# First tile after three norms from unsplit float32 products of x (1 + scale) and shift

## The chip, the cores and the metric

The kernel runs on one core of a Trainium2 chip. The metric is the time of one execution on the device in microseconds (us); a verdict compares repeated executions of the two kernels on the same chip. The core's engines work side by side and meet through semaphores: PE (matrix products, with its weight loads shown as PEld), DVE (elementwise work), ACT (elementwise work with functions), POOL, and SP, whose queue issues nearly all transfers. Each engine takes its instructions in the order of its own program. Products are summed in PSUM, eight banks of 512 float32 columns.

## The reference

A two-layer decoder trunk on 256 tokens of width 1024. Each layer has a token mixer (layer 0 a mixture of three attentions, layer 1 a gated linear attention, GLA) and a gated feed-forward part. Before each of the four sub-layers stands a norm with a shift and scale from a conditioning vector:

```python
sh1, sc1, g1, sh2, sc2, g2 = split(silu(c) @ w_ada[i] + b_ada[i])
h = rmsnorm(x, norm_mix[i]) * (1.0 + sc1) + sh1
...
x = x + g1 * y
h = rmsnorm(x, norm_ffn[i]) * (1.0 + sc2) + sh2
x = x + g2 * conv_ffn(h, w_up[i], conv_w[i], conv_b[i], w_down[i])
```

`rmsnorm(x, g)` is `x * rsqrt(mean(x * x) + eps) * g`. The mean is taken over the 1024 channels of a token, so its factor (called r below, `rstd` in the code) is one number per token. Hence, for a weight matrix W, `h @ W = r * ((x * g * (1 + sc)) @ W) + sh @ W`: the factor r can be applied before or after the product.

## The kernel before

**Layout.** Everything is channel-major: x is held as eight tiles x[kt] of 128 channels by 256 tokens, and an activation stands in the same form. A weight tile of 128x2048 (1 MB) is loaded by SP's queue into one of four buffers `raw`.

**Products in three parts.** The engine's faster float32 format (fp32r) keeps fewer bits, so each float32 operand is split in two: `split` (line 154) casts a weight tile on ACT to `whi` (two instructions of 1024 columns) and puts the rest on DVE into `wlo` (two more). There are three buffers for `whi` and three for `wlo`. `mm3` (line 171) then makes three fp32r matmuls, hi*hi, hi*lo and lo*hi, which appear in the profile as lines 174, 175 and 176. A tile of `w_up`, `w_qk_b` or `w_r_b` takes 48 matmuls of 256 columns.

**A norm.** While the last projection of a sub-layer runs, `residual` (line 271) updates x[kt] on DVE, and `add_square` (line 194) squares it on ACT and adds the squares up in three partial sums. `all_normed` (line 265) calls `rstd_of` (line 182): three matmuls with a matrix of 1/1024 sum the partial sums over the channels (`ms`), and ACT makes ln and then exp of it (`ln`, `rstd`). Behind them six matmuls of nothing (`warm`) run. `normed` (line 245) makes for each of the eight kt `xr = x * scale * r` on DVE (line 250), `hhi = xr + shift` on ACT (line 252) and `hlo`, the rest, on DVE (line 253). Then the products of the next sub-layer may start with h[0].

**Three of the norms.** Norm A stands between the output projection of the attention (`project`, line 515, tiles `py`) and the feed-forward part of layer 0; norm B between the down projection of layer 0 (tiles `pd`) and the GLA; norm C between `project` of the GLA and the feed-forward part of layer 1. The norm at the very start is another piece of code.

**Feed-forward part.** `ffn` (line 538) first makes 22 tiles of `w_up` (i = 0 to 21): 48 matmuls into one bank `pab`, then on ACT and DVE a convolution over three tokens (`r`), silu, a product and its split into `ghi` and `glo`. Every third (layer 0) or fifth (layer 1) tile brings a piece of the conditioning (`next_ada`), a 1 MB load and two long DVE reductions (`ada_raw`, line 138). Then 32 half tiles of `w_down` follow (`pd`).

**GLA.** After norm B come the values (`pv`, 96 matmuls of 512 columns over four tiles of `w_v_b`), the gate's low-rank part (`glr`, `z`) with a chain on ACT and DVE that ends in `e_q`, `e_k`, `e_d`, and per head `states` (line 673): `pqk` from one tile of `w_qk_b` (48 matmuls), then `k_d`, `q_t`, `k_t` on DVE, which need that chain, then small products `kdt`, `a`, `kv`.

**What sets the order.** The program is written in the order of the text, and a scheduler orders each engine's instructions by data, buffers and its own time estimates; `behind(...)` makes the instructions of a block follow given ones on their engine. `bank` (line 66) takes PSUM banks in a fixed rotation of three tags (p twice, s and t three times) unless a tag is given.

Of the kernel before, what the change touches and what calls it, by code (L numbers as in the profile page):

```python
# [18 lines left out]
P = 128  # L19
D = 1024  # L20
T = 256
# [36 lines left out]
def trunk(ctx: ExitStack, tc: tile.TileContext, I, out):  # L58
# [136 lines left out]
    def add_square(kt):  # L195

        sq = tmp.tile([P, T], F32, tag="sq", name="sq")
        i = nc.scalar.activation(sq, x[kt], AF.Square)
        part = 0 if kt < 3 else 1 if kt < 7 else 2
        if kt in (0, 3, 7):  # L200
            sums[part] = sq
        else:
            acc = tmp.tile([P, T], F32, tag="sqacc", name="sqacc")
            (nc.gpsimd if kt < 3 else nc.vector).tensor_tensor(acc, sums[part], sq, op=ALU.add)
            sums[part] = acc
        if kt < 6:
            squared[0] = i
# [57 lines left out]
    def all_normed(l, sub):  # L265
        r = rstd_of([sums[0], sums[1], sums[2]])
        with behind(norm_ops[0]):
            keep_warm(6)
        return [normed(l, sub, r, kt) for kt in range(KT)]

    def residual(l, sub, kt, ps):
        g = mod[l, 3 * sub + 2, kt]
        i = nc.vector.scalar_tensor_tensor(x[kt], ps, g[:, 0:1], x[kt], op0=ALU.mult, op1=ALU.add)
        if kt < 6:
            squared[1] = i
# [239 lines left out]
    def project(src, o, l, sub):  # L515

        ends = []
        for n in range(4):
# [11 lines left out]
            ends.append(e)  # L530
            for i in range(2):
                residual(l, sub, 2 * n + i, ps[i][:, T * i : T * i + T])
                add_square(2 * n + i)

    project(I["w_out_a"], o, 0, 0)
# [5 lines left out]
    def ffn(l):  # L541
        h = all_normed(l, 1)
        with tc.tile_pool(name=f"ffn{l}", bufs=2) as pool:
            g_hi = [pool.tile([P, T], F32R, tag=f"ghi{i}", name="ghi", bufs=1) for i in range(NFF)]
            g_lo = [pool.tile([P, T], F32R, tag=f"glo{i}", name="glo", bufs=1) for i in range(NFF)]
            for i in range(NFF):
                with behind(*(squared[:1], chain[3], chain[7])[min(i, 2)]):
                    w = split(I["w_up"][l, i], 2048)
                pab = bank("pab")
                pu = [pab[:, :T], pab[:, T:]]  # L550
                for kt in range(KT):
                    for s in range(2):
                        mm3(pu[s][:, :T], parts(w, 2 * P * kt + P * s), h[kt], kt == 0 and s == 0, kt == KT - 1 and s == 1)
# [37 lines left out]
    ffn(0)  # L591
# [13 lines left out]
    h = all_normed(1, 0)  # L605
# [176 lines left out]
    project(I["w_out_b"], o, 1, 0)  # L782
    gl_pool.__exit__(None, None, None)

    ffn(1)
# [141 lines left out]
```

## Time and profile before

| | |
|---|---|
| median of 3 runs | 803.75 us (802.86 to 808.61) |
| the profiled execution | 802.44 us, of which the span is 800.7 us |
| granted PE clock, mean | 0.995 of full |
| read from memory | 182.59 MB, 229 GB/s over the span |
| norm A, B, C: first matmul of `ms` | at 297.45, 485.52 and 605.26 us |
| up stage of the feed-forward part, layers 0 and 1 | from 301.47 and from 609.28 us |

The span is what the trace covers; about 1.7 us lie around it. In the views a line gives the start, the duration, the engine, the tile written and the line of the program; "x4" means four instructions drawn as one. One float32 product that isn't fp32r shows as two matmul records. The ends of matmuls are modelled, so the pace of PE is read from the distance of starts. "Idle before" names what the engine waited for.

### The profile page before, as it was taken

Reading aid. Unit: us, or ns where it says so; the run is one execution under the profiler, and the core shown is the slowest. Engines: PE = TensorE matmul, PEld = TensorE weight load, DVE = VectorE, ACT = ScalarE, POOL = GpSimd, SP = SyncE. Lnnn points to the kernel's source line nnn. Section 1 sums busy time; section 2 is a strip of 40 time slices with the busy share of each in tenths; the row PEclk is TensorE's granted clock in tenths of the full one; section 3 lists DMA queues with packets and bytes.
Section 4 is the critical chain, followed back from the end, with each engine's and each line's share of the span. In section 5 each row is a group of like instructions: output and inputs, shape, how many; then the busy total and the mean of one; then the engine's idle time right before and its main releaser. Section 6 shows DMA issues by size and latency. Waiting matters only on the chain.

```text
span 800.7 us, 15941 instructions
## 1 busy us (share of the span) xinstructions
PE 781.9 (98%) x6486; PEld 753.3 (94%) x6486; DVE 643.9 (80%) x1150; ACT 468.2 (58%) x869; POOL 15.2 (2%) x40
## 2 busy tenths in 40 slices
PE   7999999999999999999999999999999999999997
PEld 5999999999999989999999998889998999999997
DVE  6988978879778759999997877785468999988552
ACT  5556555555555546776765545744566866666442
POOL 1000000000000010000000100000010000000100
PEclk9899999999999999999999999999999999999999
DMA  8998577585685825886647793973343777644531
GB/s 343 418 334 298 202 280 278 202 329 197 248 312 200 301 85 204 301 301 223 240 162 249 268 332 127 366 261 108 106 156 109 275 269 248 251 141 159 181 110 53
DMA packets 32183, 184.72 MB, mean 231 GB/s; under 512 B 5804, under 2 KB 7340, under 8 KB 15470
## 3 DMA queue, kind: packets, MB, share of 16 engines
q1 hardware_dynamic: 32110, 183.70, 63.9%
q8 instruction: 51, 0.84, 0.4%
q14 instruction: 22, 0.18, 0.1%
HBM read 182.59 MB, written 1.10 MB: 229 GB/s over the span
## 4 chain that ended last, share of the span: by engine, by line
PE 89%; DVE 5%; DMA 3%; ACT 2%; issue 1%; SPq 0%; ACTq 0%; DVEq 0%
PE pab L176 10%; PE pab L175 10%; PE pab L174 10%; PE pqk L174 7%; PE pqk L175 6%; PE pqk L176 6%; PE pd L176 5%; PE pd L175 5%; PE pd L174 5%; PE pv L174 3%; PE pv L175 3%; PE pv L176 3%; DVE wlo L168 2%; PE py L175 2%; PE py L174 2%; PE s L367 2%
## 5 line engine op out<-in xcount | busy, mean ns | idle before, releaser
L168 DVE TENSOR_TENSOR wlo<-raw,whi 128x1024 fp32r<-128x1024 f32 (+2 forms) x274 | 295.8, 1107 | 55.6 <-ACT whi L165 54.8
L165 ACT CAST whi<-raw 128x1024 fp32r<-128x1024 f32 (+2 forms) x274 | 248.1, 954 | 152.4 <-PE pab L175 50.6
L174 PE MATMUL pab<-hhi,whi 128*128 128x256 f32 x704 | 194.0, 277 | 1.5 <-ACT hhi L252 1.5
L175 PE MATMUL pab<-hlo,whi 128*128 128x256 f32 x704 | 193.9, 276 | 0.5 <-DVE hlo L253 0.5
L176 PE MATMUL pab<-hhi,wlo 128*128 128x256 f32 x704 | 194.0, 276 | 0.4 <-DVE wlo L168 0.4
L174 PEld LDWEIGHTS pab<-hhi,whi 128*128 128x128 f32 x704 | 132.0, 188 | 2.2 <-ACT hhi L252 1.9
L175 PEld LDWEIGHTS pab<-hlo,whi 128*128 128x128 f32 x704 | 132.0, 188 | 0.9 <-DVE hlo L253 0.9
L176 PEld LDWEIGHTS pab<-hhi,wlo 128*128 128x128 f32 x704 | 132.0, 188 | 0.8 <-DVE wlo L168 0.8
L174 PE MATMUL pqk<-hhi,whi 128*128 128x256 f32 x448 | 123.5, 287 | 3.7 <-ACT hhi L252 3.2
L175 PE MATMUL pqk<-hlo,whi 128*128 128x256 f32 x448 | 125.0, 283 | 0.0
L176 PE MATMUL pqk<-hhi,wlo 128*128 128x256 f32 x448 | 124.9, 283 | 0.0
L138 DVE CUSTOM_DVE_ANT_0 ada_raw<-ada_raw,c_bc 128x1024 f32<-128x1024 f32 x96 | 113.5, 1218 | 4.5 <-DMA ada_raw<-in_w_ada 4.4
L176 PE MATMUL pd<-ghi,wlo 128*128 128x256 f32 x352 | 98.0, 280 | 0.6 <-DVE wlo L168 0.6
L175 PE MATMUL pd<-glo,whi 128*128 128x256 f32 x352 | 98.1, 280 | 0.0
L174 PE MATMUL pd<-ghi,whi 128*128 128x256 f32 x352 | 97.7, 279 | 0.0
L174 PEld LDWEIGHTS pqk<-hhi,whi 128*128 128x128 f32 x448 | 83.7, 191 | 5.5 <-ACT hhi L252 3.7
L175 PEld LDWEIGHTS pqk<-hlo,whi 128*128 128x128 f32 x448 | 85.0, 190 | 0.4
L176 PEld LDWEIGHTS pqk<-hhi,wlo 128*128 128x128 f32 x448 | 84.9, 190 | 0.2
L176 PEld LDWEIGHTS pd<-ghi,wlo 128*128 128x128 f32 x352 | 65.8, 187 | 0.8 <-DVE wlo L168 0.8
L175 PEld LDWEIGHTS pd<-glo,whi 128*128 128x128 f32 x352 | 66.0, 188 | 0.0
L174 PEld LDWEIGHTS pd<-ghi,whi 128*128 128x128 f32 x352 | 65.9, 188 | 0.0
L560 ACT ACTIVATE r<-pab,small 128x256 f32<-128x256 f32 x88 | 48.5, 559 | 11.7 <-DVE r L563 11.3
(184 smaller groups left out, 1248.2 us busy)
## 6 DMA issues: line engine op xcount, KB each, us to landing
ada_raw<-in_w_ada SPq DMA_DIRECT2D x47, 1024.0 KB, 6.7
raw<-in_w_up SPq DMA_DIRECT2D x44, 1024.0 KB, 5.2
raw<-in_w_down SPq DMA_DIRECT2D x32, 704.0 KB, 4.2
raw<-in_wqk SPq DMA_DIRECT2D x18, 1024.0 KB, 7.2
raw<-in_wv SPq DMA_DIRECT2D x14, 768.0 KB, 4.6
raw<-in_w SPq DMA_DIRECT2D x7, 960.0 KB, 6.6
raw<-in_w_out_a SPq DMA_DIRECT2D x4, 1024.0 KB, 6.9
raw<-in_w_v_b SPq DMA_DIRECT2D x4, 1024.0 KB, 6.7
```

The lines of the kernel that those rows point to most:

```text
L138: nc.vector.tensor_tensor_reduce(w, w, c_bc, op0=ALU.mult, op1=ALU.add, scale=1.0, scalar=0.0, accum_out=dot,)
L165: copied[0] = nc.scalar.copy(hi[:, c], raw[:, c])
L168: last_lo[0] = nc.vector.tensor_tensor(lo[:, c], raw[:, c], hi[:, c].bitcast(F32), op=ALU.subtract)
L174: mm(ps, a[0], b[0], start=start, stop=False)
L175: mm(ps, a[0], b[1], start=False, stop=False)
L176: return mm(ps, a[1], b[0], start=False, stop=stop)
L367: mm(s[:, 0:n], q[0][a][:, r].rearrange("p a b -> p (a b)"), k[0][b][:, 0:n], start=(i == 0), stop=(i == 2))
L560: nc.scalar.activation(r, u[:, :T], AF.Identity, scale=cw[2], bias=col(C_CB + 44 * l + f))
```

## The change

For the first tile after norms A, B and C the product is made from x itself, before r is known. As each x[kt] is updated, ACT also writes `early_x[kt]`: its first 256 columns are x * scale (`scale`), and column 256 is the shift (`shift_columns`, written at some earlier time). The tile's raw float32 weights are loaded without a split (`load_early`). PE makes 16 plain float32 products of 257 columns (`products`), two per kt, into two banks: four of them ahead of the `ms` matmuls, twelve behind them, where the six `warm` matmuls stood. `whole` applies r on DVE and adds the last column, the product with the shift, on ACT as a bias.

In `ffn` the first tile (i = 0) comes out of this, without its split and its 48 matmuls; the splits of tiles 1, 2 and 3 are put behind h[0], h[5] and h[7], where before tile 0 was only behind an earlier square, tile 1 behind h[3] and the rest behind h[7]. In the GLA the first tile is the first head's q and k; the splits of the `w_v_b` tiles 0 and 1 are put behind h[0] and h[5], where tile 0 was only behind earlier squares and residuals. The `ms` matmuls now use tag p and the early banks tags s and t (or t twice), so the rotation for all later banks starts elsewhere. The reserve for DMA descriptors in SBUF goes to 4096.

```diff
             acc = tmp.tile([P, T], F32, tag="sqacc", name="sqacc")
-            (nc.gpsimd if kt < 3 else nc.vector).tensor_tensor(acc, sums[part], sq, op=ALU.add)
+            last_sum[:] = [(nc.gpsimd if kt < 3 else nc.vector).tensor_tensor(acc, sums[part], sq, op=ALU.add)]
...
-    def all_normed(l, sub):
-        r = rstd_of([sums[0], sums[1], sums[2]])
+    early_x = [state.tile([P, T + 16], F32, tag=f"ex{k}", name="early_x") for k in range(KT)]
+    last_x, last_sum = [], []
+
+    def shift_columns(l, sub):
+        with behind(*chain[7]):
+            for kt in range(KT):
+                nc.scalar.copy(early_x[kt][:, T : T + 1], mod[l, 3 * sub, kt])
+
+    def scale(l, sub, kt):
+        return nc.scalar.mul(early_x[kt][:, 0:T], x[kt], mod[l, 3 * sub + 1, kt][:, 0:1])
+
+    def load_early(src):
+        early = wraw.tile([P, 2048], F32, tag="raw", name="raw")
+        nc.sync.dma_start(early, src)
+        return early
+
+    def all_normed(l, sub, tags, early):
+        ps = [bank("early", t) for t in tags]
+
+        def products(tiles):
+            for kt in tiles:
+                for s in range(2):
+                    mm(ps[s][:, 0 : T + 1], early[:, 2 * P * kt + P * s : 2 * P * kt + P * s + P], early_x[kt][:, 0 : T + 1],
+                       start=(kt == 0), stop=(kt == KT - 1))
+
+        products(range(2))
+        r = rstd_of([sums[0], sums[1], sums[2]], tag="p")
         with behind(norm_ops[0]):
-            keep_warm(6)
-        return [normed(l, sub, r, kt) for kt in range(KT)]
+            products(range(2, KT))
+
+        def whole(s, out):
+            dot = tmp.tile([P, 1], F32, tag="dot", name="dot", bufs=4)
+            nc.scalar.copy(dot, ps[s][:, T : T + 1])
+            nc.vector.tensor_tensor(out, ps[s][:, 0:T], r, op=ALU.mult)
+            nc.scalar.activation(out, out, AF.Identity, bias=dot[:, 0:1])
+            return out
+
+        return [normed(l, sub, r, kt) for kt in range(KT)], whole
...
-        i = nc.vector.scalar_tensor_tensor(x[kt], ps, g[:, 0:1], x[kt], op0=ALU.mult, op1=ALU.add)
+        with behind(*(last_sum if kt == 7 else ())):
+            i = nc.vector.scalar_tensor_tensor(x[kt], ps, g[:, 0:1], x[kt], op0=ALU.mult, op1=ALU.add)
...
     def project(src, o, l, sub):
+        shift_columns(l, 1)
...
+            if n == 3:
+                early = load_early(I["w_up"][l, 0])
             for i in range(2):
                 residual(l, sub, 2 * n + i, ps[i][:, T * i : T * i + T])
                 add_square(2 * n + i)
+                scale(l, 1, 2 * n + i)
+        return early
...
-        h = all_normed(l, 1)
+        h, whole = all_normed(l, 1, "st", early)
...
             for i in range(NFF):
-                with behind(*(squared[:1], chain[3], chain[7])[min(i, 2)]):
-                    w = split(I["w_up"][l, i], 2048)
-                pab = bank("pab")
-                pu = [pab[:, :T], pab[:, T:]]
-                for kt in range(KT):
+                if i == 0:
+                    with behind(*chain[5]):
+                        pu = [whole(s, pool.tile([P, T], F32, tag="u", name="u")) for s in range(2)]
+                else:
+                    with behind(*((), chain[0], chain[5], chain[7])[min(i, 3)]):
+                        w = split(I["w_up"][l, i], 2048)
+                    pab = bank("pab")
+                    pu = [pab[:, :T], pab[:, T:]]
+                for kt in range(KT if i else 0):
...
+            if l == 0:
+                shift_columns(1, 0)
...
+                early = load_early(I["w_qk_b"][0]) if (l, f2) == (0, 6) else None
                 for f in range(2):
                     residual(l, 1, f2 + f, pd[f][:, :T])
                     add_square(f2 + f)
+                    if l == 0:
+                        scale(1, 0, f2 + f)
...
-    h = all_normed(1, 0)
+    h, whole = all_normed(1, 0, "tt", early)
...
-        with behind(*(squared, chain[5], chain[7], glr_copy)[n]):
+        with behind(*(chain[0], chain[5], chain[7], glr_copy)[n]):
             w = split(I["w_v_b"][n], 2048)
...
+        if n == 0:
+            with behind(*chain[7]):
+                qk0 = gt([P, 2, T], "qk0")
+                for s in range(2):
+                    whole(s, qk0[:, s, :])
...
     def states(hd):
-        w = split(I["w_qk_b"][hd], 2048)
-        pqk = bank("pqk", "p")
-        pq, pk = pqk[:, :T], pqk[:, T:]
-        for kt in range(KT):
-            mm3(pq, parts(w, 2 * P * kt), h[kt], kt == 0, False)
-            mm3(pk, parts(w, 2 * P * kt + P), h[kt], False, kt == KT - 1)
+        if hd == 0:
+            pq, pk = qk0[:, 0, :], qk0[:, 1, :]
+        else:
+            w = split(I["w_qk_b"][hd], 2048)
+            pqk = bank("pqk", "p")
+            pq, pk = pqk[:, :T], pqk[:, T:]
+            for kt in range(KT):
+                mm3(pq, parts(w, 2 * P * kt), h[kt], kt == 0, False)
+                mm3(pk, parts(w, 2 * P * kt + P), h[kt], False, kt == KT - 1)
...
-    nc = bacc.Bacc("TRN2", target_bir_lowering=False, num_devices=1)
+    nc = bacc.Bacc("TRN2", target_bir_lowering=False, num_devices=1, dynamic_dma_scratch_size=4096)
```

More of the change, by code (lines that the diff above doesn't have):

```diff
@@ L533, in project, with ffn @@
                 add_square(2 * n + i)
-    project(I["w_out_a"], o, 0, 0)
+                scale(l, 1, 2 * n + i)
+        return early
+    early = project(I["w_out_a"], o, 0, 0)
     at_pool.__exit__(None, None, None)
     last_pd = [None]
-    def ffn(l):
-        h = all_normed(l, 1)
+    def ffn(l, early):
+        h, whole = all_normed(l, 1, "st", early)
         with tc.tile_pool(name=f"ffn{l}", bufs=2) as pool:
@@ L589, in ffn @@
                         next_ada()
-    ffn(0)
+        return early
+    early = ffn(0, early)
     gl_pool = tc.tile_pool(name="gla", bufs=1)
@@ L781, in trunk @@
     exp_ln_after(last_hi)
-    project(I["w_out_b"], o, 1, 0)
+    early = project(I["w_out_b"], o, 1, 0)
     gl_pool.__exit__(None, None, None)
-    ffn(1)
+    ffn(1, early)
     halves = [slice(P * t, P * t + P) for t in range(2)]
```

## The prediction

> **What bounds the kernel now.** I read the page first, then busy time by windows around the norms, the chain of waits, and the timelines of DVE and ACT.
>
> ```profile
> span 800.7 us, 15941 instructions
> PE 781.9 (98%) x6486; PEld 753.3 (94%) x6486; DVE 643.9 (80%) x1150; ACT 468.2 (58%) x869; POOL 15.2 (2%) x40
> PE 89%; DVE 5%; DMA 3%; ACT 2%; issue 1%; SPq 0%; ACTq 0%; DVEq 0%
> ```
>
> PE carries 89% of the chain that ended last, so nearly everything is PE's own pace, and a gain can only come from holes in PE's work or from less of it. The windows (PE, PEld, DVE, ACT, POOL, then clock, DMA share, GB/s) show both sides of the matter:
>
> ```profile
> 297.40:301.40 4.00, 3.11 (x20) 2.41 (x19) 1.53 (x5) 1.80 (x5) 0.00 (x0) 1.00 0.78 262
> 605.20:609.20 4.00, 3.12 (x20) 2.41 (x19) 1.74 (x5) 1.79 (x5) 0.00 (x0) 1.00 0.74 248
> 308.00:320.00 12.00, 12.00 (x108) 12.00 (x108) 11.42 (x16) 8.33 (x12) 0.00 (x0) 1.00 0.84 298
> ```
>
> In the 4 us at norms A and C PE issues 20 records, twelve of them the fillers: that time is to be had. But right behind norm A DVE works 11.42 of 12 us. The chain there says the same:
>
> ```profile
> 297.65 0.50 DVE x_all L273
> 298.23 0.42 ACT sq L198
> 298.69 0.71 PE ms L186 x2
> 299.43 0.48 ACT ln L188
> 299.94 0.43 ACT rstd L190
> 300.39 1.28 DVE xr L250 x3
> 301.67 0.79 DVE hlo L253 x2
> ...
> 304.44 1.17 DVE wlo L168
> 305.66 0.39 PE pab L176
> ```
>
> From the last residual to 305.66 the chain never rests on PE's work except for `ms`; from 300.39 on it is DVE, with h's halves and the split of the next weight tile, that sets the pace. So two things must be priced: PE's work, and how early DVE can feed it afterwards.
>
> **The change, PE's side (norms A and C).**
>
> ```profile
> 297.45 1.03 PE L186 MATMUL ms<-sqacc,ones_d 128*128 128x256 f32 x4
> 485.52 1.03 PE L186 MATMUL ms<-sqacc,ones_d 128*128 128x256 f32 x4
> 605.26 1.03 PE L186 MATMUL ms<-sqacc,ones_d 128*128 128x256 f32 x4
> L186 PE MATMUL ms<-sqacc,ones_d 128*128 128x256 f32 x12 | 3.1, 379 | 0.0
> 546.56 0.43 PE ms L186 x2
> 533.34 0.42 PE kv L706 x2
> 299.23 1.50 PE L263 MATMUL warm<-ones_d 128*128 128x128 f32 x12
> 301.40:305.60 4.20, 3.73 (x26) 1.00 0.00 0
> 305.60:320.00 14.40, 14.34 (x126) 1.00 0.70 248
> 613.47 0.38 PE pab L176
> ```
>
> The first three rows give E, where the old work ends: A 297.45, B 485.52, C 605.26. A plain float32 product of 256 columns is two records and takes 0.43 us in the chain. The two windows hold `pab` records alone: 14.40/126 = 0.114 us per fp32r matmul, 5.5 us per tile of 48. So the early tile costs 16 x 0.43 = 6.9 us in place of 5.5: 1.4 us more work per norm. The 257th column has no row: between nothing (1 column in 256) and the 0.12 us per record of the third rival; I take nothing, as the rows show time going with columns.
>
> The group view's mean of 379 ns per record would make the 32 records 12.1 us, 5.2 more per norm. [...]
>
> Before: at 305.66 PE has done 26 of the 144 matmuls of tiles 0 to 2, and runs without a hole from there: tile 2 ends at 305.66 + 118 x 0.114 = 319.1, E + 21.7. For C, taken alike from 613.47, it is 626.9, E + 21.7 too.
> After, PE alone: three `ms` products (1.3) and the early ones (6.9) put the start of tile 1 at E + 8.2 = 305.6; tiles 1 and 2 need 96 x 0.114 = 10.9, so E + 19.1. PE's own gain is 2.6 us.
>
> **What DVE and ACT leave of it.** The changed order of instructions puts on ACT: hhi0, whi of tile 1 (two), hhi1 to hhi5, two one-column copies, whi of tile 2 (two), hhi6, two biases, hhi7; on DVE: xr0 to 2, hlo0, xr3, wlo of tile 1 (two), hlo1 to 3, xr4 to 6, hlo4, hlo5, the two products with r, xr7, wlo of tile 2 (two), hlo6, hlo7.
>
> ```profile
> 303.30 1.98 ACT L165 CAST whi<-raw 128x1024 fp32r<-128x1024 f32 x2
> 305.19 1.35 ACT L252 ACTIVATE hhi<-xr,mod 128x256 fp32r<-128x256 f32 x3
> 323.56 0.28 ACT L148 ACTIVATE mod<-dot,small 128x1 f32<-128x1 f32 x1
> 309.70 1.22 DVE L138 CUSTOM_DVE_ANT_0 ada_raw<-ada_raw,c_bc 128x1024 f32<-128x1024 f32 x1
> 311.99 4.62 DVE L168 TENSOR_TENSOR wlo<-raw,whi 128x1024 fp32r<-128x1024 f32 x4
> ```
>
> With 1.0 per whi, 0.45 per hhi, 1.14 per wlo, 0.40 per xr and hlo (chain rows above), for A:
> the four products ahead of `ms` move its last matmul from 298.69 to E + 1.72 + 0.86 = 300.0, so r and xr0 come 1.3 us later, at 301.7 (at A one of the four stands a little earlier, within `py`; the sum is the same). xr0 to 2 and hlo0 to 303.3, xr3 303.7, wlo 306.0, hlo1 to 3 307.2, xr4 to 6 308.4, hlo4 and 5 309.2, products with r 310.0, xr7 310.4, wlo 312.7, hlo6 313.1, hlo7 313.5. On ACT hhi5, after xr5 at 308.0, ends at 308.6, the one-column copies (0.2 each of the 0.28 shown, as neighbours on ACT overlap by some 0.1) at 309.0, whi at 311.0, hhi6 at 311.5.
> PE, from 305.6 at 0.68 per kt: hlo4 (308.8) costs 0.3; six kt are done at 310.1; two matmuls of tile 2, then it stands until hhi6 at 311.5, 1.2 us; 57 matmuls remain: 311.7 + 6.5 = 318.2. Gain at A 0.9 us, at C the same by the same order: 1.8 together. Tile 3 starts at 318.2 and its wlo, behind hlo7 and an `ada_raw` pair (2.3), has its first half at 317.0: on time, by 1.2.
>
> Costed at nothing: the removed fillers (in a hole); the removed split of tile 0 (done ahead of E); 24 scalings, 0.42 each like `sq`, on an ACT that is 58% busy (scaling of x7 ends before the later `ms` does; without this cover 0.4 per norm); 24 column copies in earlier stages (24 x 0.2 = 5 us of ACT, on the path only where ACT is the limit); the rotation of banks (a wait for one would cost a DVE step of 0.4); the smaller descriptor reserve (SP issues the transfers before and after). Transfers:
>
> ```profile
> 266.68 8.72 SPq L159 DMA_DIRECT2D raw<-in_w_up  x3
> 297.13 15.29 SPq L159 DMA_DIRECT2D raw<-in_w_up  x3
> raw<-in_w_up SPq DMA_DIRECT2D x44, 1024.0 KB, 5.2
> ```
>
> Tiles 0 to 2 are there long before E. Tile 3's load was issued at 297.13, when wlo of tile 0 freed its buffer; now the early weights hold that buffer until 305.6, SP's queue waits there with tiles 4 and 5 behind, and the load lands at 310.8: ACT is with hhi7 until 312.9, so it is hidden by 2 us.
>
> **GLA (norm B).**
>
> ```profile
> 489.49 0.50 PE pv L174
> 489.99 0.23 PE pv L175
> 509.42 1.92 PE z L625 x8
> 526.48 0.12 PE pqk L175
> 529.10 0.41 DVE k_d L682
> PE kdt L690 <- DVE k_d L682: 1.4, 1, 1.4
> ```
>
> Before, PE is dense from 489.6 and does 96 `pv` (0.23), 24 `glr`, `z` (1.9) and heads 0 and 1 (96 x 0.117): 38 us, to 527.6. Then it waits for k_d, 529.5; with head 2 (5.6) it stands at 535.1.
> After, the same list with heads 1 and 2 starts at E + 8.2 = 493.7 and ends at 531.7: 3.4 earlier at equal work. But `z` ends after 70 `pv` and `glr`, 493.7 + 16.1 + 2.7 + 1.9 = 514.4, where it was 511.3. k_d came 17.8 after `z`; kept, that is 532.2. The new order also puts an `ada_raw` pair ahead of `dl`, and two wlo (2.3) between k_t and k_d: bounds 532.2 and 532.2 + 4.6 = 536.8. I take 533.4 for its start, nearer the lower end, which is the measured row; the added DVE work partly falls where DVE waited for ACT's functions. PE then goes on at 533.8 and has nothing to do while ACT copies kdT (0.6, estimated as a 256-column step like `rstd`, 0.43, and the matmul's way to it): 534.4. Gain 0.7; at the bounds 1.9 and -2.7.
>
> **Sum.** 0.9 + 0.9 + 0.7 = 2.5. The profiled execution took 802.44 (1.7 around its span) and would take 799.9; the median of the runs is 1.3 above it: 803.75 - 2.5 = 801.3.
>
> **Rivals.**
> *DVE and ACT hold nobody up* (their queues run ahead of my sum): PE's own gains, 2.6 + 2.6 + 3.4 = 8.6, 795.2. For it: the hole that I place hangs on a few tenths at hhi4, hhi5 and whi. Against: 11.42 of 12 us busy. 14%.
> *A new wait in the GLA*: k_d comes at the upper bound, 536.8, and PE goes on at 537.2 + 0.6, 2.7 later than before; with 1.8 gained at A and C that is 803.75 + 0.9 = 804.7. It turns the sign once k_d starts after 535.9. For it: the measured 1.4 us wait on just this, and a gate chain that starts 3.1 later. Against: PE itself comes there later. 18%.
> *The unsplit weights don't load behind the products.* Every early record has new weights; 32 loads showing 0.12 us each (an estimate: 1.50/12, the pace of the fillers with their loads) cost 3.8 per norm: 803.75 - 2.5 + 11.5 = 812.8. From 0.03 us per record the gain is gone. An odd column count with a price of its own would act alike. Against: the `kv` row, new weights each, 0.21 per record. [...] 7%.
> *The change doesn't do what it says* (the scheduler puts the products late): in the changed order they stand directly behind the old work, one even within it. 3%, 803.8.
>
> **How the numbers follow.** My forecast has 58%, with its own range 799 to 804. Fast beyond 1% (below 795.7; the runs shown scatter by 0.7%, so 1% is about what can be told) is half of the first rival: 7%. Slow beyond 1% (above 811.8) is the third: 7%. The rest, 86%, is within 1%. The range 796.5 to 806.5 leaves out half of the first rival, the third, and the end of the second: some 16% with scatter.
>
> **What would show it.** `ms` of the last square 1.3 us later after E; 32 early records at 0.215; PE's last filler gone; a wait of `pab` L174 on hhi of about 1 us, twice; `kdt` waiting on k_d for 1 to 2 us; clock still 1.00. I am wrong if the early records stand wider, if holes appear in tiles 3 to 6 of the up stage (DVE never recovers), or if k_d comes after 536.

## The result and the profile after

Ten runs of the changed kernel have a median of 800.26 us (798.38 to 803.31), ten of the kernel before on the same chip 803.7 us (801.1 to 808.61). The ratio is 0.9961 with a 95% interval of 0.9943 to 0.9979, that is 3.1 us less (1.7 to 4.6), where 2.5 less was predicted. The profiled execution took 798.48 us.

The page of the changed kernel (its line 291 holds the early products, 302 the product with r, 743 k_d, 751 the transposes kdt, 767 kv):

```profile
span 796.4 us, 15793 instructions
PE 779.3 (98%) x6402; PEld 748.8 (94%) x6402; DVE 637.8 (80%) x1150; ACT 477.1 (60%) x923; POOL 16.5 (2%) x40
PE 70%; DVE 14%; DMA 8%; ACT 5%; issue 2%; SPq 0%; ACTq 0%; DVEq 0%
```

The windows that answer to the three of before: 4 us from the last `py` at A and at C, and 12 us further on (PE, PEld, DVE, ACT, POOL, then clock, DMA share, GB/s).

```profile
296.30:300.30 4.00, 4.00 (x21) 3.52 (x20) 0.69 (x2) 1.71 (x4) 0.00 (x0) 1.00 0.00 0
601.96:605.96 4.00, 4.00 (x21) 3.52 (x21) 0.48 (x1) 1.51 (x4) 0.00 (x0) 1.00 0.00 0
305.00:317.00 12.00, 11.50 (x94) 10.90 (x94) 12.00 (x22) 10.37 (x24) 0.00 (x0) 1.00 0.85 304
```

The hole at the norm is full of products. Behind it DVE works 12.00 of 12 us, and PE gets 94 matmuls in where it had 108: DVE and ACT now hold it up. The chain of waits at C shows at which step (start, us, what):

```profile
612.27 0.91 ACT hhi L252 x2
613.18 0.10 ACT dot L301 x2
613.29 1.90 ACT whi L165 x2
615.18 0.41 ACT hhi L252
615.60 0.04 issue
615.64 0.39 PE pab L174
```

It is hhi of kt 6 behind the two casts of tile 2, as the prediction had it. The sequence ahead of it is the predicted one too: r's first user `xr` starts 4.30 us after the last `py` at C, 3.06 before. The list of PE's waits has that step at both norms, and the two that were forecast for B:

```profile
PE kdt L751 <- DVE k_d L743: 1.5, 1, 1.5
PE pab L174 <- ACT hhi L252: 0.8, 2, 0.4
PE kv L767 <- ACT kdT L752: 0.5, 1, 0.5
```

By the modelled ends PE waits 0.4 us for hhi at each norm; by the distance of starts it loses 1.0 there. What the early products cost stands in the groups and in the chain:

```profile
L291 PE MATMUL early<-early_x,raw 128*128 128x257 f32 x96 | 21.9, 380 | 0.0
```

```profile
484.87 5.20 PE early L291 x24
```

5.20/24 = 0.217 us per record. The mean of 380 ns in the group line would have been wrong by three quarters.

Where the time went, read from first and last matmuls of each stage (us). "Again" is the same changed kernel profiled a second time.

| stage | before | after | again |
|---|---|---|---|
| start to last `py` of A | 297.32 | 296.23 | 297.43 |
| A: last `py` to last `pab` | 125.07 | 123.58 | 123.58 |
| down, layer 0 (first to last `pd`) | 62.90 | 61.64 | 63.08 |
| B: last `pd` to last `pr` | 97.23 | 97.71 | 96.17 |
| `py` of the GLA | 22.39 | 22.50 | 22.50 |
| C: last `py` to last `pab` | 125.07 | 124.01 | 124.02 |
| down, layer 1 | 62.07 | 62.07 | 62.07 |
| span | 800.7 | 796.4 | 797.5 |

A and C repeat to a hundredth. B and the down stage of layer 0 differ between two executions of one program by 1.5 us, more than the whole change is worth at one norm. That had to be explained before B could be judged.

### The profile page after: what moved, and what is told of

It reads as the page before. It is cut to its first block, busy times and chain, and to the rows that moved or that the text cites. A ratio compares the mean times of both kernels' runs of the same rounds, so it can differ in the third digit from the quotient of the medians.

```text
span 796.4 us, 15793 instructions
## 1 busy us (share of the span) xinstructions
PE 779.3 (98%) x6402; PEld 748.8 (94%) x6402; DVE 637.8 (80%) x1150; ACT 477.1 (60%) x923; POOL 16.5 (2%) x40
## 4 chain that ended last, share of the span: by engine, by line
PE 70%; DVE 14%; DMA 8%; ACT 5%; issue 2%; SPq 0%; ACTq 0%; DVEq 0%
PE pab L176 9%; PE pab L174 9%; PE pab L175 9%; DVE wlo L168 5%; PE pd L174 5%; PE pd L175 5%; PE pd L176 5%; DMA raw<-in_wqk 4%; DVE ada_raw L138 3%; DMA raw<-in_wv 2%; PE pqk L176 2%; PE pqk L175 2%; PE pqk L174 2%; ACT whi L165 2%; PE py L174 2%
## 5 line engine op out<-in xcount | busy, mean ns | idle before, releaser
L165 ACT CAST whi<-raw 128x1024 fp32r<-128x1024 f32 (+2 forms) x268 | 242.1, 952 | 151.8 <-PE pab L175 49.7
L168 DVE TENSOR_TENSOR wlo<-raw,whi 128x1024 fp32r<-128x1024 f32 (+2 forms) x268 | 287.7, 1101 | 49.3 <-ACT whi L165 48.3
L174 PE MATMUL pab<-hhi,whi 128*128 128x256 f32 x672 | 186.1, 277 | 0.8 <-ACT hhi L252 0.8
L175 PE MATMUL pab<-hlo,whi 128*128 128x256 f32 x672 | 185.9, 277 | 0.1
L176 PE MATMUL pab<-hhi,wlo 128*128 128x256 f32 x672 | 185.7, 276 | 0.1
L174 PEld LDWEIGHTS pab<-hhi,whi 128*128 128x128 f32 x672 | 126.2, 188 | 1.3 <-ACT hhi L252 1.2
L175 PEld LDWEIGHTS pab<-hlo,whi 128*128 128x128 f32 x672 | 126.2, 188 | 0.7 <-DVE hlo L253 0.4
L176 PEld LDWEIGHTS pab<-hhi,wlo 128*128 128x128 f32 x672 | 126.2, 188 | 0.5 <-DVE wlo L168 0.5
L174 PE MATMUL pqk<-hhi,whi 128*128 128x256 f32 x432 | 118.1, 285 | 3.9 <-ACT hhi L252 3.4
L175 PE MATMUL pv<-wlo,hhi 128*128 128x384 f32 (+1 forms) x144 | 49.9, 350 | 0.0
```

Of the source, the lines that this page charges most:

```text
L165: copied[0] = nc.scalar.copy(hi[:, c], raw[:, c])
L168: last_lo[0] = nc.vector.tensor_tensor(lo[:, c], raw[:, c], hi[:, c].bitcast(F32), op=ALU.subtract)
L174: mm(ps, a[0], b[0], start=start, stop=False)
L175: mm(ps, a[0], b[1], start=False, stop=False)
L176: return mm(ps, a[1], b[0], start=False, stop=stop)
```

## Experiments

### Norm B as before

```diff
-    h, whole = all_normed(1, 0, "tt", early)
+    r = rstd_of([sums[0], sums[1], sums[2]])
+    with behind(norm_ops[0]):
+        keep_warm(6)
+    h = [normed(1, 0, r, kt) for kt in range(KT)]
...
-        if hd == 0:
-            pq, pk = qk0[:, 0, :], qk0[:, 1, :]
-        else:
-            w = split(I["w_qk_b"][hd], 2048)
+        w = split(I["w_qk_b"][hd], 2048)
```

The scalings of x, the shift columns, the early load and the order of the splits at B are put back as well.

> The changed kernel with norm B put back as it was (fillers, head 0's q and k from a split tile); A and C keep the early tile. Stage B is read from the last pd of layer 0 to the last pr: 97.2 us before the change, 97.7 after it. Theory 1 (the early tile at B is worth nothing: what PE gains it gives back at the wait for k_d): stage B 97.2, the time equal to the changed kernel's 800.3 or 0.5 below. Theory 2 (B gained 0.7 as predicted, and the 3.5 us at half clock that the changed kernel's profile shows behind that wait were chance): stage B 97.2 here, but up to 1.2 longer than in changed kernels without such a spell; the time 0.7 to 1.2 above 800.3. At A and C both expect what the changed kernel shows: tile 2 of the up stage starts 14.9 and 15.3 us after the last py.

Stage B took 98.80 us, longer than with the early tile (97.71), though k_d came 43.69 us after the last `pd` and not 48.31. The ratio to the kernel before was 0.9955 (0.9924 to 0.9987), on this count no different from the changed kernel. The clock tells why the stage is long (windows of this kernel, then of the first trace of the changed one, columns as above):

```profile
530.00:532.00 2.00, 1.16 (x5) 0.92 (x6) 2.00 (x7) 1.45 (x3) 0.00 (x0) 0.83 0.98 401
532.00:534.00 2.00, 2.00 (x11) 2.00 (x10) 2.00 (x3) 0.00 (x0) 0.00 (x0) 0.50 1.01 397
534.00:536.00 2.00, 2.00 (x13) 1.79 (x13) 2.00 (x5) 0.00 (x0) 0.00 (x0) 0.82 0.80 213
```

```profile
530.00:532.00 2.00, 1.20 (x8) 0.88 (x8) 2.00 (x5) 0.67 (x2) 0.00 (x0) 1.00 1.00 377
532.00:534.00 2.00, 2.00 (x9) 1.47 (x8) 2.00 (x6) 1.38 (x5) 0.00 (x0) 0.50 0.91 369
534.00:536.00 2.00, 2.00 (x14) 2.00 (x13) 2.00 (x2) 0.00 (x0) 0.00 (x0) 0.65 0.85 233
```

In both, the granted clock falls to 0.50 for some 3.4 us right behind the wait for k_d. The trace of the kernel before had that wait (1.4 us) and no such spell (clock 1.00 from 528 to 545 us). So the early tile at B is not what brings the spell, and stage B has to be compared with like: 97.23 before against 96.17 (again) without a spell, 98.80 against 97.71 with one. Both ways the early tile at B is worth 1.1 us up to the last `pr`. Neither theory gave the 98.80, since the spell came here too; the second has the gain right.

Read on to the last `py`, the gain is 1.0 without a spell (119.74 before, 118.78 again) and 1.8 with one (122.12 here, 120.32 in the first trace). Without the early tile PE waits 0.4 for `olo` at the first `py`; in the two traces of the changed kernel it doesn't, but there `py` takes 118 ns per matmul, against 113 in the trace of before. Other kernels with the early tile do wait at that place (next section), so this part of the gain is not sure.

### The next tile split ahead of the norm (A and C)

```diff
-                    with behind(*((), chain[0], chain[5], chain[7])[min(i, 3)]):
+                    with behind(*((), squared[:1], chain[5], chain[7])[min(i, 3)]):
```

> At A and C the split of up tile 1 (two casts on ACT, two wlo on DVE) goes ahead of the norm, where tile 0's split was before the change; B as in the changed kernel. Theory (DVE and ACT, busy with that split behind the norm, make hhi of kt 6 late and leave PE a hole of 1.7 us in tile 1): the hole goes, tile 2 starts 13.2 (A) and 13.8 us (C) after the last py in place of 14.9 and 15.3, and the time is some 3.2 below the changed kernel's 800.3: 797.1. Rival (the hole comes from r being late, by the four products ahead of ms): tile 2 still at about 14.5 and 15.0, time 799.5 or more. Second rival (the split ahead of the norm only delays the last x): the gain comes back as a later last ms, 800.3.

Tile 2 started 13.37 us (A) and 14.00 us (C) after the last `py`, against 14.89 and 15.33. The chain of this kernel at C holds no step of ACT or DVE any more:

```profile
607.87 3.47 PE early L291 x16
611.33 0.12 PE pab L174
611.45 0.12 PE pab L175
```

So the hole was DVE's and ACT's, and its price was 1.3 to 1.5 us, as predicted (0.3 + 1.2). But the time did not follow: the ratio was 0.9976 (0.9939 to 1.0012), no better than the changed kernel's. Two dense windows of the up stages, layer 0 and layer 1, show what came in between:

```profile
330.00:410.00 80.00, 80.00 (x708) 80.00 (x707) 77.27 (x138) 56.08 (x100) 0.00 (x0) 1.00 0.70 243
640.00:720.00 80.00, 80.00 (x682) 80.00 (x680) 73.28 (x132) 53.57 (x96) 0.00 (x0) 1.00 0.61 210
```

PE is busy for all of 80 us and the clock is 1.00 in both, yet it makes 708 matmuls in one and 682 in the other: 113 and 117 ns each. In starts, a tile of 48 takes 5.44 us or 5.655, from the first tile to the last. Over the 20 tiles that are left of an up stage that is 4.3 us, which is more than the gain of both norms.

This kernel differs at one more place, which the edit didn't touch. The scheduler's order in the GLA is another one: the `ln` of the last head stands behind two casts of `whi` that wait for PE's gate products, so the last head's output is late (chain of waits):

```profile
573.39 2.00 ACT whi L165 x2
575.87 0.39 ACT ln L188
580.70 0.43 DVE olo L840
581.17 0.39 PE py L175
```

PE waits 0.5 for `ohi` and 0.7 for `olo` there, and the last `py` comes 121.54 us after the last `pd`, 1.2 later than in the changed kernel's first trace (120.32). Four kernels below have these waits too: the split ahead with a forced break, the fillers, the first break in the down stage, and all together.

### All early products behind `ms`

```diff
-        products(range(2))
         r = rstd_of([sums[0], sums[1], sums[2]], tag="p")
         with behind(norm_ops[0]):
-            products(range(2, KT))
+            products(range(KT))
```

> All 16 early products stand behind the ms matmuls, none ahead, at all three norms. Theory (DVE and ACT behind r set the pace at A and C): r comes 1.3 us sooner, PE stands 0.4 us more ahead of the last ms, tile 2 starts 0.9 sooner after the last py (14.0 to 14.4), stage B is 0.4 longer; the time 1.4 below 800.3: 798.9. Rival (PE's own work sets the pace, the products ahead are cover that is worth 0.4 us at each norm): tile 2 starts 0.4 later at A and C, stage B 0.4 longer, the time 1.2 above: 801.5.

Neither time was right: the ratio was 1.0057 (1.0028 to 1.0085), by the ratios some 7 us more than the changed kernel. The near part went as the theory had it: tile 1 without a hole, tile 2 at 14.49 in both layers, sooner by 0.4 and 0.8 (0.9 was expected; the longer pace takes 0.2 within tile 1). Then both up stages ran at 5.655 us per tile:

```profile
330.00:410.00 80.00, 80.00 (x682) 80.00 (x681) 73.47 (x129) 53.19 (x96) 0.00 (x0) 1.00 0.69 243
640.00:720.00 80.00, 80.00 (x682) 80.00 (x681) 73.47 (x133) 51.89 (x93) 0.00 (x0) 1.00 0.61 218
```

They ended 127.44 us after the last `py`, 3.9 and 3.4 later than in the changed kernel. Stage B grew by 1.4 (99.13, with a spell at clock 0.50 for 3.4 us): 0.4 at its start as expected, the rest behind k_d, which came 2.5 later.

This gave a new theory: PE has two paces, keeps the one that it has while it runs dense, and settles anew at a break. By it the holes that the change leaves in tile 1 had done some good.

### The same with a forced break

```diff
+                        if i in (2,) and l in (0, 1) and kt == s == 0:
+                            mm(pu[0][:, :T], a[0], b[0], start=True, stop=False)
+                            nc.gpsimd.tensor_copy(a[0][:, 0:1], a[0][:, 0:1].bitcast(F32))
+                            held = (mm(pu[0][:, :T], a[0], b[1], start=False, stop=False),)
...
+                        with behind(*held):
+                            mm3(pu[s][:, :T], a, b, kt == 0 and s == 0, kt == KT - 1 and s == 1)
```

> The kernel with all early products behind ms, which had no hole in up tile 1 and ran the whole of both up stages at 117.7 ns from one matmul to the next (5.655 us per tile) where the changed kernel, which has holes in tile 1, runs at 113.3 (5.44 per tile). New: in tile 2 of both layers POOL copies one column of whi onto itself behind the tile's first matmul, and the second waits for it, so PE gets one hole of about 0.5 us. Theory (PE has two paces, it keeps the one it has while it runs without a break, and a break of some tenths lets it settle in the faster one): tiles 3 to 21 take 5.44 us each in both layers, 0.215 x 19 = 4.1 us less each, minus the hole; last pab some 123.9 after the last py in place of 127.44; the time 7 us below that kernel's 810.7, about 803.5. Rival (the slower pace comes from the order of work or the place of the banks, not from a missing break): 5.655 per tile as before, the time 0.5 to 1 above 810.7.

The timeline of PE in this kernel shows the break, the windows what follows it:

```profile
310.18 0.28 PE L603 MATMUL pab<-hhi,whi 128*128 128x256 f32 x1
310.30 0.28 PE L174 MATMUL pab<-hhi,whi 128*128 128x256 f32 x1
311.22 0.39 PE L605 MATMUL pab<-hlo,whi 128*128 128x256 f32 x1 [0.64 <-POOL whi L604]
```

```profile
330.00:410.00 80.00, 80.00 (x708) 80.00 (x708) 76.80 (x136) 56.15 (x101) 0.00 (x0) 1.00 0.70 244
640.00:720.00 80.00, 80.00 (x709) 80.00 (x708) 75.54 (x137) 54.19 (x97) 0.00 (x0) 1.00 0.61 214
```

The last `pab` came 124.07 us after the last `py` in both layers, 3.4 sooner than without the break and 0.2 from the expected value. The traced run, 801.54 us, was the shortest of its twelve; their median was 805.44 (803.5 expected), the ratio 1.0019 (0.9996 to 1.0042). The break helps, but not as surely as this one trace would have it.

### The changed kernel again

> The changed kernel once more, unaltered, on the same chip as the other runs. All theories: tile 2 starts 14.9 (A) and 15.3 us (C) after the last py, both up stages at 5.44 us per tile, a wait of 1.4 to 2.2 us of kdt for k_d; the ratio to the kernel before near 0.996. What may differ from the first trace: the down stage of layer 0 (61.6 or 62.9 us by the pace that PE has there) and whether a spell at half clock follows the wait for k_d.

As expected in A and C (table above), with no spell at half clock (1.00 from 533 to 539 us) and the longer down stage. The ratio was 0.9974 (0.9946 to 1.0002), median 802.18: a gain of 2.1 us, less than the 3.1 of the result, and no gain at all is just within the interval.

### The split ahead and a forced break

The edits of two experiments above, joined:

```diff
+                    with behind(*((), squared[:1], chain[5], chain[7])[min(i, 3)]):
...
+                        if i in (2,) and l in (0, 1) and kt == s == 0:
...
```

> The kernel with up tile 1 split ahead of the norm (tile 2 started at 13.4 and 14.0 us after the last py, but layer 1's up stage then ran at 5.655 us per tile), with the same forced hole of about 0.5 us in tile 2 of both layers. Theory of the two paces: both up stages at 5.44 per tile from tile 3 on, last pab 122.6 (A) and 123.1 (C) after the last py, where the changed kernel has 123.6 and 124.0; the time 1.9 us below the changed kernel's in this call. Rival (the pace follows from the order of the work): layer 1 stays at 5.655, last pab 127.4 there, the time 3 above the changed kernel's.

Last `pab` at 122.64 and 123.08: the stages are as expected to a tenth, 0.9 us shorter each than the changed kernel's. The traced run took 798.64 us, again the shortest of twelve. Their median was 803.87 us, 1.7 above the changed kernel's 802.18 where 1.9 below was expected, and the ratio 0.9999 (0.9971 to 1.0027): over many runs the gain did not show. Part of the reason stands in the trace: from the last `pd` of layer 0 to the last `py` of the GLA it took 121.48, 1.2 more than the changed kernel's first trace, by the waits for `ohi` and `olo` described above.

### Fillers in the wait for k_d

```diff
+        if hd == 0:
+            with behind(a):
+                for i in range(6):
+                    last = (mm(ps[:, T : T + P], ones_d, ones_d, start=True, stop=True),)
...
         for t in range(2):
+            with behind(*last):
...
```

> The changed kernel with six products of nothing (0.125 us per record, two records each) on PE between head 0's a and kdt, where PE waits 1.5 us for k_d; nothing else moves. Theory (the idle stretch there lets the granted clock fall to a half for 3.5 us, which costs 1.75): no stretch at half clock between 526 and 540, stage B (last pd of layer 0 to last pr) about 96.0 in place of 97.7, the time up to 1.7 below the changed kernel's in this call. Rival (the spell comes from the whole of the half-empty stretch up to kv, or from chance): the spell is there all the same, stage B 97.7 to 98.2, the time unchanged.

No spell (clock 1.00 from 530 to 536 us), stage B 96.38, the ratio 0.9976 (0.9948 to 1.0003), median 801.18, 1.0 below the changed kernel's of the section before last. It fits the theory, but the changed kernel's second trace had no spell without fillers either (96.17). Over all traces whose GLA is the changed kernel's, the spell was there in 4 of 6, and in 0 of 2 with fillers: a hint, not a proof. Nor did the shorter stage B reach the next stage: with the waits for `ohi` and `olo` the last `py` came 120.75 us after the last `pd`, no sooner than in the first trace with its spell (120.32).

### The first gate tile ahead of the heads

```diff
-    s0 = states(0)
+    gate(0, "s"); s0 = states(0)
...
-    gate(0)
     next_ada()
     output(3, *s3)
```

> In the GLA the first gate tile (48 pr matmuls, 5.5 us of PE that need no gate chain) is moved from behind the heads to ahead of head 0's states, into another bank; the order on DVE up to k_d stays. Theory 1 (B's gain is given back because PE has nothing to do while it waits for k_d, and the half-empty stretch there lets the granted clock fall to a half): no wait for k_d, no spell at half clock near 532 to 535, stage B (last pd of layer 0 to last pr) 94 to 95 us in place of 97.7, the time 2.5 to 4 below 800.3. Theory 2 (the chain of k_d, kdT, kv and the states sets the length of the GLA whatever PE does meanwhile): the holes come back later among kv and o, stage B within 0.7 of 97.7, the time as the changed kernel's.

The wait for k_d was gone, the last `pr` came 93.32 us after the last `pd`, 4.4 sooner. But the first `py` came at 100.67 in place of 97.83. The timeline of PE in this kernel:

```profile
576.26 0.59 PE L186 MATMUL ms<-oacc,ones_d 128*128 128x256 f32 x2
583.49 1.01 PE L174 MATMUL py<-ohi,whi 128*128 128x256 f32 x3 [6.63 <-ACT ohi L839]
```

The clock fell with it, to a half for 10.2 us (window as above):

```profile
583.00:589.00 6.00, 5.24 (x23) 4.95 (x24) 4.07 (x13) 3.86 (x10) 0.00 (x0) 0.50 0.14 60
```

The gate tile was what PE did while the last head's output was made ready. Moved forward, it leaves a wait of 6.6 us there. And k_d came at the same 48.31 us, but PE, busy with the moved tile's work, took it up 2.0 later, and the first `kv` came 53.83 us after the last `pd` in place of 49.68. That the chain from k_d to the outputs sets the length of the GLA, the second theory, fits this best; neither theory had a stage B of 93.3. The ratio was 1.0013 (0.998 to 1.0047).

### A break in the down stage, twice tried

```diff
+                        if (f2, half, f, j) in ((0, 0, 1, 3),):
+                            mm(pd[f][:, :T], a[0], b[0], start=False, stop=False)
+                            nc.gpsimd.tensor_copy(a[0][:, 0:1], a[0][:, 0:1].bitcast(F32))
+                            held = (mm(pd[f][:, :T], a[0], b[1], start=False, stop=False),)
...
```

> The changed kernel, with one forced hole of some 0.6 us (the same column copy on POOL) in the second of the 16 weight tiles of the down stage, in both layers. Layer 1's down stage (first to last pd) took 62.07 us in every trace so far, all at 117.7 ns per matmul; layer 0's 63.1 or 61.6, where a wait for a weight cast at 440 us brought the faster pace in 5 traces of 10. Theory (any break lets PE settle anew, in the faster pace more often than not): with the hole layer 1's down stage runs at 113.3 from the second tile on, 62.07 + 0.6 - 2.1 = 60.6 us, and layer 0's about 61.4 (it has waits of its own); if the break fails to change the pace, 62.7. Rival (in the down stages another thing, such as waits on the weight loads, sets the pace): 62.7 in both. The time: 1.5 to 3 below the changed kernel's by the theory, 1.2 above it by the rival.

It tested nothing: PE had 22 other matmuls to do between the first product and the one that waits, and no break arose. Layer 1's stage stayed at 62.07, and the ratio was 1.0017 (0.9978 to 1.0056). But the trace showed two things. In layer 0, A's up stage ran at 5.655 per tile from tile 2 on, behind the very holes that had brought 5.44 in the traces of the changed kernel. And a row of waits for the split weights in the down stage (446 to 450 us) was followed by half clock (0.50 for 3.4 us from 450 us), 66.12 us for the stage.

The second try has breaks in two tiles, and `held` applies to all that follows in the stage:

```diff
-                    held = ()
+                    held = () if (f2, half, f) == (0, 0, 0) else held
...
-                        if (f2, half, f, j) in ((0, 0, 1, 3),):
+                        if (f2, half, f, j) in ((0, 0, 1, 3), (2, 0, 1, 3)):
```

> The changed kernel with two forced breaks in the down stage of both layers (in the second and the sixth of its 16 weight tiles), this time with all later products of the stage held behind them, so that PE cannot fill them (in the earlier kernel it filled its one break, and the stage stayed at 62.07 us). Theory (each break draws PE's pace anew, 113.3 or 117.7 ns; without one it never changes): layer 1's down stage, 62.07 at 117.7 in all traces so far, has at least one change of pace, or at two draws of the slower pace costs just the breaks, some 1.2; from the break at which the faster pace is drawn, every tile takes 33 x 4.4 ns = 0.145 us less, so 62.07 + 1.2 - 2.0 = 61.3 if the first draws it, 61.8 if the second does, 63.3 if none. Rival (the down stage cannot run at 113.3, since its waits or loads set the pace): 63.3 with 117.7 throughout.

Here the breaks came. Layer 1 in the timeline of PE and in windows between the two breaks and behind the second:

```profile
756.10 0.28 PE L634 MATMUL pd<-ghi,whi 128*128 128x256 f32 x1
756.92 0.38 PE L636 MATMUL pd<-glo,whi 128*128 128x256 f32 x1 [0.55 <-POOL whi L635]
```

```profile
741.00:755.00 14.00, 14.00 (x121) 14.00 (x120) 8.05 (x13) 7.76 (x12) 1.19 (x1) 1.00 0.50 162
758.00:772.00 14.00, 14.00 (x126) 14.00 (x126) 6.29 (x9) 7.12 (x12) 1.18 (x1) 1.00 0.55 176
```

Behind the first break PE stayed at 118 ns, behind the second it ran at 113: 62.14 us for the stage with two breaks of 0.8. So the down stage can run at 113, and a break can change the pace or leave it. In layer 0 the first break brought 113, two waits at 445 to 447 us brought 118 back, and the second forced break left it at 118. The ratio was 0.9987 (0.9959 to 1.0015).

### All together

The split ahead, the forced break in up tile 2 and the fillers, each as above, and the first of the two edits of the down stage.

> All together: up tile 1 split ahead of the norm at A and C, a forced hole in up tile 2 and in the second tile of the down stage of both layers, and the fillers in the wait for k_d. Theory: up stages as in the kernel with the split ahead and the hole (last pab 122.6 and 123.1 us after the last py), no spell at half clock behind k_d (stage B 96.2 to 96.4), down stages 60.6 to 61.4: in the trace 0.9 + 0.9 + 1.4 + 1.4 = 4 to 4.6 us less than a changed kernel with that spell, the ratio to the kernel before about 0.992. Rival (the gains of single stages are lost in the paces that the rest falls into, attention and GLA among them): stages as said, but the ratio no better than the changed kernel's 0.996.

The ratio was 0.9971 (0.9936 to 1.0007), median 803.07 us: in the time the rival, no better than the changed kernel. In the traced run, the longest of its twelve (808.78 us), both up stages ran at 5.655 per tile in spite of the forced breaks, which neither theory nor rival had. In the down stage no break arose, as in the first try above, so only its up stages and its GLA (96.31, no spell) count.

### Breaks further back in the up stage

The kernel with all early products behind `ms`, and:

```diff
-                        if i in (2,) and l in (0, 1) and kt == s == 0:
+                        if i in (8, 15) and l in (0, 1) and kt == s == 0:
```

> The kernel with all early products behind ms (no break in the up stage, 5.655 us per tile all through, in both layers) with forced breaks of about 0.5 us in tiles 8 and 15 of both up stages. Theory (the pace is drawn at a break and kept): tiles 1 to 7 at 5.655, and the pace changes at tile 8 or at tile 15 and nowhere else; with the draws seen in the up stages so far (the faster pace in 17 of 20 stages with a break) at least three of the four stretches behind a break run at 5.44. Rival (the pace follows from what comes ahead of the stage): 5.655 in all tiles. The time between 803.5 and 811.5 by the draws.

Again no break arose, since other products of the tile were ready and POOL was done in time:

```profile
345.17 0.28 PE L603 MATMUL pab<-hhi,whi 128*128 128x256 f32 x1
345.29 0.28 PE L174 MATMUL pab<-hhi,whi 128*128 128x256 f32 x1
```

All tiles took 5.65 us in both layers, the ratio was 1.0059 (1.003 to 1.0089). It repeats the kernel without breaks, to the hundredth: 127.44 and 127.44. Whether a break in the middle of an up stage changes its pace is thus not tested.

## Why the prediction was right, and where it was not

**Norms A and C: right in the steps.** The early tile ends 8.16 us after the last `py` at C (8.2 predicted), and 7.73 at A, where one of its products stands within `py`. r comes 1.24 later at C (1.3). Tile 1 takes 7.17 us at C in place of 5.44: 1.7 us of holes, 1.5 predicted, of them 1.0 at hhi of kt 6 (1.2) and 0.3 at hlo of kt 4 (0.3). No hole is seen in tiles 3 to 6. What remains is 1.06 at C and 1.49 at A; less the 0.43 of the product that stands within `py` it is 1.06 at A too, where 0.9 was predicted for each. The row that priced it best was the chain's 0.43 for two `ms` records. The first rival, that DVE and ACT hold nobody up, fell with the hole in tile 1, which goes only when the split is put ahead. The third, exposed weight loads, fell with 0.217 us per record.

**Norm B: the waits are the predicted ones, the gain came out near by two errors that offset each other.** k_d came 48.31 us after the last `pd` (48.0 predicted), `kv` stood 0.5 for kdT (0.6). Between like traces the gain up to the last `pr` is 1.1, where 0.7 was predicted. But the forecast's own step, the start of `kv`, came at 49.7 us after the last `pd`, where 49.0 was forecast: by the sum as it stands nothing would have been gained. The sum left out the small products. At 49.7 us PE in the trace of before has done some 26 matmuls of the heads less than the changed kernel, head 0 counted in (3.1 us), but 1.7 us more of `a`, `kdt` and `kv`, and it is this difference that the sum doesn't hold. The second rival, k_d at its upper bound, did not come: k_d stood 20.95 us behind the start of `z`, 19.75 before, and those 1.2 are what was taken between the bounds. The row that it was taken from holds only roughly: in the kernel with norm B as before `z` came 0.7 sooner than in the trace of before, and k_d no sooner.

**Costed at nothing.** The down stage of layer 0 took 63.08 against 62.90 in traces at the same pace. The scalings of x for norm B are not the reason: the kernel with norm B as before has none there and took 63.09. What differs is the one wait of the stage, 0.7 for `whi` in place of 0.6 for `wlo`; why it changed is open. No wait of PE in the trace points to one of the other items, but none of them was tested alone.

**The sum.** In the second trace the up and down stages have the paces of the trace of before, and there is no spell behind k_d either. Its span is 3.2 us shorter: 1.5 at A, 1.1 at B and 1.05 at C. From these 3.6 go 0.5, by which the two `py` stages and the down stage of layer 0 grew, and the attention ahead of A adds 0.1. The first trace's 4.3 differs from that by 1.4 less in the down stage, where PE went over to 113 ns at 440 us, 1.5 more at B for the spell, and 1.2 less up to the last `py` of A.

**What the prediction did not see.** It took 0.114 us per matmul as the price of fp32r work in the up stage (0.117 for the heads of the GLA), and 1.00 for the clock. Neither is fixed. The windows of the trace of before held both paces already (80 us of layer 0's up stage, 55 us of its down stage):

```profile
330.00:410.00 80.00, 80.00 (x708) 80.00 (x707) 77.62 (x138) 57.34 (x101) 0.00 (x0) 1.00 0.69 240
425.00:480.00 55.00, 54.44 (x463) 54.23 (x462) 42.40 (x66) 28.97 (x51) 2.23 (x2) 1.00 0.82 292
```

54.44/463 = 118 ns in the second. The step between the two paces falls on the first product of the down stage, 0.11 us after the last `pab`, with no idle time and no other work of PE between. Windows of 20 us on both sides of it:

```profile
402.00:422.00 20.00, 20.00 (x179) 20.00 (x178) 19.42 (x38) 13.28 (x27) 0.00 (x0) 1.00 0.42 146
423.00:443.00 20.00, 20.00 (x172) 20.00 (x171) 15.38 (x29) 12.49 (x23) 0.21 (x1) 1.00 0.68 246
```

All 19 up stages at 113 ns end so, and each of the 28 down stages starts at 118. So the theory of the experiments, that PE keeps its pace as long as it runs without a break, holds within a stage and fails at this border.

By the forecast's terms the kernel with all early products behind `ms` had to gain over the change, and it lost 7 us to it. And two kernels whose up stages are the changed kernel's, those with a break in the down stage alone, ran A at 118 ns: 127.86 in place of 123.58. That would have turned the sign of the forecast. That the changed kernel has 113 ns in both of its traces was luck as far as the forecast goes, since its sum holds no reason for it.

**What stays open.** Of 22 up stages with a break in tiles 0 to 2, 18 ran at 113 ns; of 6 without, 1. The same up stage gave both at A, 113 in five traces and 118 in two; but these are traces of six programs that differ further on, and the only one traced twice had 113 both times in its up stages, and both paces only in the down stage of layer 0. So the traces leave open whether an up stage's pace is drawn anew in each execution or goes with the program. The run times point to a draw in some programs: those of "All together" spread from 798.48 to 808.78 us, with both up stages at 118 ns in the longest, and those of the split ahead, which has no break in its up stages, from 800.86 to 810.68. But the 22 runs of the two kernels with all early products behind `ms` and no break lie between 808.68 and 813.48. What decides the pace is not known, nor whether the change moved the odds against the kernel before, of which there is one trace. The slow paces of two stages may not be one thing: in the first trace of the changed kernel every third weight load of the GLA's `py`, at 118 ns, lasts 192 ns, and in its down stage of layer 1, at 118 ns too, none does (187 or 188).

That the scatter of the runs (798 to 814 us over all kernels) comes from these paces is argued from the spans of the traces: 796.4 to 803.1 with both up stages at 113 ns, 800.2 to 807.8 with one, 806.8 to 808.0 with none. It can't be all of it, since the stretch up to the last `py` of A alone took from 296.23 to 299.65.

## What to carry to other kernels

Before a difference of a few microseconds is explained, count the matmuls in a dense window of each stage in both traces, and read the granted clock behind each wait: a stage of a thousand matmuls moved by 4 us with neither its code nor its work changed. Compare stages only between traces that agree in both. An edit can also reorder work far from its place: compare the order of the other engines too. And work moved into a wait is a gain only if it wasn't covering another wait where it stood.

## What the hardware showed unexpectedly

PE at full granted clock showed two paces for dense fp32r matmuls of 256 columns with a new weight load each, 113.3 and 117.8 ns from start to start (5.44 and 5.655 us per 48). Within an up or a down stage it kept its pace for up to 119 us without a break (21 tiles at 5.655, with all early products behind `ms`) and changed it, either way, only at breaks. From the up stage to the down stage it went from 113 to 118 ns without one, in all 19 cases. The cause is open.

A spell at half clock followed a wait far shorter than itself. In the changed kernel's first trace PE was busy for 1.42 of the 3.4 us ahead of the drop, its longest idle stretch there, the wait for k_d, was 1.5 us, and the clock then stood at 0.50 for 3.4 us, some 1.5 us of time. With the same GLA the spell came in 4 traces of 6. The second trace of the same program had the longer wait for k_d, 1.9 us, and no spell (clock 1.00 from 533 to 539 us). What decides it is not shown.
